# Which block of rows a partition takes: 4q+b takes 32b+q in place of 4q+b

## The chip, the core and the metric

The kernel runs on one core of one Trainium2 chip. The metric is the device time of one execution in microseconds (us), taken on the chip. Beside it stands a profile of one execution, in which every instruction of the engines and every packet of the DMA engines has its times. The engines used are VectorE (DVE), ScalarE (ACT), GpSimd (POOL, for constants and the end only) and SyncE (SP), which issues DMAs. TensorE does nothing here.

## The reference

The input has 32 x 512 rows of 1024 floats, and each row is summed:

```python
x = np.random.randn(32, 512, 1024).astype(np.float32)

def reference(x):
    return np.sum(x, axis=-1).astype(np.float32)
```

That is 16,384 sums over 67.1 MB that have to be read once. The output is 64 KB.

## The kernel before

The 16,384 rows are split over 128 partitions, J = 128 rows for each (lines 115 to 128). The split has two regions. The first P * BIG = 2,048 rows are region a: partition p takes BIG = 16 consecutive rows. The other 14,336 rows are region b: partition p takes LONG = 112 consecutive rows, a block of 448 KB. So consecutive partitions read places 448 KB apart in region b and 64 KB apart in region a. `rows_from` (line 131) gives the source of a load of n rows per partition from row j on: region b for j under 112, region a from there.

A load brings n rows of every partition into a tile of 16 rows (64 KB) per partition; the pool `in` has three such tiles. `rows` (line 188) issues one load on SP's queue and the sums that belong to it. The order is written out by hand (`manual_schedule`), and it is this:

1. One load of FIRST = 7 rows from region b, which `issue_first_load_at_entry` (line 10) moves to the very entry of the program, ahead of the barrier at which the engines meet.
2. Seven loads of 16 rows (line 215): the one of region a first, then region b at rows 16, 32, up to 96. The first of them is held until a tiny ACT instruction has run (line 222), the second until DVE has summed the first load (line 224). From the third on a load waits for a tile to come free.
3. The remaining rows 7 to 15 of region b: a load of 6 rows, one of 2, and the last row in two pieces of 560 and 464 floats (lines 227 to 237), each by a DMA of its own.

The sums land in a tile `sums` of 128 x 128, one column for each row of a partition. Most loads are summed by one DVE instruction over the tile (`vec`, line 151). The last ones are summed row by row, on DVE by an instruction that adds the two halves of a row and accumulates (`halves`, line 164), and on ACT by a copy that accumulates (`act`, line 177).

Three stores bring `sums` out. ACT's queue issues columns 16 to 111 (region b) and columns 112 to 127 (region a), both held until the two-row load has been summed (lines 239 and 240). SP's queue issues columns 0 to 15 of region b last (line 243), after the last sum. `wait_for_the_store_at_the_clear` (line 55) puts the wait for that last store at the instruction that clears the semaphores at the very end, on POOL. `order_waits` (line 31) only sorts the waits of an instruction that has several.

The change touches the views `x_a`, `x_b`, `out_b` and the loads and stores that use them.

Of the kernel before, what the change touches and what calls it, by code (L numbers as in the profile page):

```python
# [100 lines left out]
@with_exitstack  # L101
def kernel(
    ctx: ExitStack,
    tc: tile.TileContext,
    x: bass.AP,
    out: bass.AP,
):
    nc = tc.nc
    nc.at_finalize(issue_first_load_at_entry)
    nc.at_finalize(order_waits)  # L110
    nc.at_finalize(wait_for_the_store_at_the_clear)
    fp32 = mybir.dt.float32
    P = 128
    batch, seq, dim = x.shape
    rows = batch * seq
    J = rows // P
    BIG = 16

    LONG = J - BIG
    rows_in = x.flatten_outer_dims()
    rows_out = out.rearrange("b s -> (b s)")
    x_a = rows_in[: P * BIG].rearrange("(p j) d -> p j d", p=P)
    x_b = rows_in[P * BIG :].rearrange("(p j) d -> p j d", p=P)
    out_a = rows_out[: P * BIG].rearrange("(p j) -> p j", p=P)
    out_b = rows_out[P * BIG :].rearrange("(p j) -> p j", p=P)


    def rows_from(j, n):
        return x_b[:, j : j + n, :] if j < LONG else x_a[:, j - LONG : j - LONG + n, :]

    last = 0
    FIRST = 7
    pieces = (560, 464)
    LINE = 64

    with (
        tc.tile_pool(name="small", bufs=1) as smallpool,  # L140
        tc.tile_pool(name="in", bufs=3) as inpool,
        tc.tile_pool(name="unread", bufs=4, space=bass.MemoryType.PSUM) as upool,
        tc.tile_pool(name="stage", bufs=1) as stpool,
        tc.manual_schedule(),
    ):


        seed = smallpool.tile([P, LINE // 2], fp32)
        sums = stpool.tile([P, J], fp32)

        def vec(dst, src):
            return nc.vector.tensor_reduce(  # L152
                out=dst, in_=src, axis=mybir.AxisListType.X, op=mybir.AluOpType.add
            )

        def hold(inst, until, reason):
            tc.add_manual_dep(
                inst.ins,
                until.ins.name,
                mybir.DependencyInfo(mybir.DependencyClass.Sync, mybir.DependencyReason.DATA),  # L160
                reason=reason,
            )

        def halves(dst, src):
            n = src.shape[-1] // 2
            return nc.vector.tensor_tensor_reduce(  # L166
                out=src[:, :n],
                in0=src[:, :n],
                in1=src[:, n:],
                scale=1.0,  # L170
                scalar=0.0,
                op0=mybir.AluOpType.add,
                op1=mybir.AluOpType.add,
                accum_out=dst,
            )

        def act(dst, src, n):
            unread = upool.tile([P, dim], fp32)
            nc.scalar.activation(  # L179
                out=unread[:, :n],  # L180
                in_=src,
                func=mybir.ActivationFunctionType.Copy,
                accum_out=dst,
            )

        sums_of = []

        def rows(t, a, n, j, n_act, pairs=False):
            nv = n - n_act
            block = t[:, a * dim : (a + n) * dim].rearrange("p (n d) -> p n d", d=dim)  # L190
            load = nc.sync.dma_start(out=block, in_=rows_from(j, n))  # L191
            if pairs:
                for q in range(nv):
                    sums_of.append(halves(sums[:, j + q : j + q + 1], block[:, q, :]))
            else:
                sums_of.append(vec(sums[:, j : j + nv], block[:, :nv, :]))
            for q in range(nv, n):
                act(sums[:, j + q : j + q + 1], block[:, q, :], dim)
            return load

        def store(eng, dst, j0, j1):
            return eng.dma_start(out=dst, in_=sums[:, j0:j1])

        nc.vector.memset(seed[:, :1], 0.0)  # L204
        unread = upool.tile([P, dim], fp32)
        ready = nc.scalar.activation(  # L206
            out=unread[:, :1], in_=seed[:, :1], func=mybir.ActivationFunctionType.Copy
        )

        j = last  # L210
        t = inpool.tile([P, BIG * dim + LINE], fp32)
        rows(t, 0, FIRST, j, 0)
        first = sums_of[-1]
        wholes = [LONG, *range(BIG, LONG, BIG)]
        for k, at in enumerate(wholes):
            t = inpool.tile([P, BIG * dim + LINE], fp32)
            if k < len(wholes) - 1:
                load = rows(t, 0, BIG, at, 0)
            else:
                rows(t, 0, BIG, at, 7, pairs=True)  # L220
            if k == 0:
                hold(load, ready, "no second load while the first one's descriptors are made")
            if k == 1:
                hold(load, first, "no descriptors of later loads while the first ones start")

        t = inpool.tile([P, BIG * dim + LINE], fp32)
        rows(t, FIRST, 6, j + FIRST, 2, pairs=True)
        two = rows(t, FIRST + 6, 2, j + FIRST + 6, 1, pairs=True)
        a = BIG - 1

        j += a
        c, width = pieces
        whole = t[:, a * dim + c : BIG * dim + 2]
        nc.vector.memset(whole[:, width + 1 :], 0.0)  # L234
        part = t[:, a * dim : a * dim + c]
        nc.sync.dma_start(out=part, in_=rows_from(j, 1)[:, 0, :c])  # L236
        nc.sync.dma_start(out=whole[:, :width], in_=rows_from(j, 1)[:, 0, c:])
        late = "its packets come behind those of the loads"
        hold(store(nc.scalar, out_b[:, BIG:], BIG, LONG), two, late)
        hold(store(nc.scalar, out_a, LONG, J), two, late)  # L240
        halves(whole[:, width : width + 1], part)
        halves(sums[:, j : j + 1], whole)
        store(nc.sync, out_b[:, :BIG], 0, BIG)


# [28 lines left out]
```

## Time and profile before

| | |
|---|---|
| median of 3 runs | 161.14 us (161.13 to 161.27) |
| span of the profiled execution, first to last instruction | 159.5 us |
| median less that span, taken for what lies around it | 1.6 us |
| DVE busy | 120.6 us (76%) |
| ACT busy | 12.1 us (8%) |
| POOL busy | 0.2 us |
| read from memory | 67.11 MB, 421 GB/s over the span |
| chain that ended last | DMA 71%, DVE 27% |

The runs give times without a profile; the profiled execution has its span alone, which starts with SP's first DMA issue. A DMA has three times: the issue on the engine that starts it (SPq and ACTq in the views), its packets on the 16 DMA engines, and its landing, when its semaphore has its full count and a waiting engine goes on. In the views a windows row gives a stretch of the span with the busy time of each engine, the share of the 16 DMA engines' time that packets took (a packet is counted where it begins, so short stretches can pass 1) and the GB/s. The chain of work lists what the end of the program waited for, back to the start. Where DVE waits, the view puts it down to the DMA that it waited for.

### The profile page before, as it was taken

Reading aid. Unit: us, or ns where it says so; the run is one execution under the profiler, and the core shown is the slowest. Engines: PE = TensorE matmul, PEld = TensorE weight load, DVE = VectorE, ACT = ScalarE, POOL = GpSimd, SP = SyncE. Lnnn points to the kernel's source line nnn. Section 1 sums busy time; section 2 is a strip of 40 time slices with the busy share of each in tenths; the row PEclk is TensorE's granted clock in tenths of the full one; section 3 lists DMA queues with packets and bytes.
Section 4 is the critical chain, followed back from the end, with each engine's and each line's share of the span. In section 5 each row is a group of like instructions: output and inputs, shape, how many; then the busy total and the mean of one; then the engine's idle time right before and its main releaser. Section 6 shows DMA issues by size and latency. Waiting matters only on the chain.

```text
span 159.5 us, 135 instructions
## 1 busy us (share of the span) xinstructions
DVE 120.6 (76%) x41; ACT 12.1 (8%) x22; POOL 0.2 (0%) x4
## 2 busy tenths in 40 slices
DVE  0029600499995999769996899949999499994955
ACT  3000000000000000000000000000000000003993
POOL 0000000000000000000000000000000000000000
DMA  8899899699699699699699798996996996996993
GB/s 302 388 493 526 362 427 526 296 493 526 263 526 526 263 526 526 263 526 493 296 526 444 345 526 378 411 526 296 493 526 263 526 526 263 526 526 265 425 382 128
DMA packets 2160, 67.18 MB, mean 421 GB/s; under 512 B 624, under 2 KB 752, under 8 KB 880
## 3 DMA queue, kind: packets, MB, share of 16 engines
q1 hardware_dynamic: 1872, 67.12, 97.8%
q10 hardware_dynamic: 288, 0.06, 0.2%
HBM read 67.11 MB, written 0.07 MB: 421 GB/s over the span
## 4 chain that ended last, share of the span: by engine, by line
DMA 71%; DVE 27%; SPq 1%; issue 0%; DVEq 0%
DMA t<-in_x_dram 71%; DVE sums L152 26%; SPq L191 0%; SPq L236 0%; DVE t L166 0%; DVEq L269 0%
## 5 line engine op out<-in xcount | busy, mean ns | idle before, releaser
L152 DVE TENSOR_REDUCE sums<-t 128x16 f32<-128x16384 f32 (+1 forms) x7 | 110.9, 15849 | 32.3 <-DMA t<-in_x_dram 32.3
L179 ACT ACTIVATE unread<-t 128x1024 f32<-128x1024 f32 x10 | 10.1, 1011 | 144.3 <-DMA t<-in_x_dram 144.3
L166 DVE CUSTOM_DVE_ANT_0 t<-t 128x512 f32<-128x512 f32 (+2 forms) x16 | 9.6, 654 | 4.0 <-DMA t<-in_x_dram 4.0
L179 ACT ACTIVATION_READ_ACCUMULATOR unread<-t 128x1 f32 x10 | 1.9, 188 | 0.0
L206 ACT ACT_TABLE_LOAD x1 | 1.3, 1283 | 0.8 <-PEq L258 0.8
L166 DVE DVE_READ_ACCUMULATOR2_ANT sums<- 128x1 f32 x15 | 1.2, 82 | 0.0
L204 DVE MEMSET seed<- 128x1 f32 x1 | 0.1, 59 | 0.8 <-PEq L258 0.8
L206 ACT ACTIVATE unread<-seed 128x1 f32<-128x1 f32 x1 | 0.2, 174 | 0.0
L258 POOL MEMSET const-bfloat16-1.0<- 128x1 bf16 x1 | 0.1, 102 | 0.0
L258 POOL MEMSET const-uint8-127<- 128x1 uint8 x1 | 0.1, 102 | 0.0
L258 POOL MEMSET const-float32-0.0<- 128x1 f32 x1 | 0.1, 99 | 0.2 <-issue 0.2
L258 POOL MEMSET const-float32-1.0<- 128x1 f32 x1 | 0.1, 99 | 0.0
L166 DVE DVE_READ_ACCUMULATOR2_ANT t<- 128x1 f32 x1 | 0.1, 83 | 0.0
L234 DVE MEMSET t<- 128x1 f32 x1 | 0.1, 59 | 0.0
## 6 DMA issues: line engine op xcount, KB each, us to landing
t<-in_x_dram SPq DMA_DIRECT2D x1, 3584.0 KB, 11.0
t<-in_x_dram SPq DMA_DIRECT2D x1, 3072.0 KB, 28.7
t<-in_x_dram SPq DMA_DIRECT2D x1, 1024.0 KB, 30.7
t<-in_x_dram SPq DMA_DIRECT2D x1, 280.0 KB, 31.0
t<-in_x_dram SPq DMA_DIRECT2D x1, 232.0 KB, 31.1
t<-in_x_dram SPq DMA_DIRECT2D x7, 40.7
out_dram<-sums ACTq DMA_DIRECT2D x1, 48.0 KB, 1.6
out_dram<-sums ACTq DMA_DIRECT2D x1, 8.0 KB, 1.6
```

The costliest lines, as they stand in the source:

```text
L152: return nc.vector.tensor_reduce(out=dst, in_=src, axis=mybir.AxisListType.X, op=mybir.AluOpType.add)
L166: return nc.vector.tensor_tensor_reduce(out=src[:, :n], in0=src[:, :n], in1=src[:, n:], scale=1.0, scalar=0.0, op0=mybir.AluOpType.add, op ...
L179: nc.scalar.activation(out=unread[:, :n], in_=src, func=mybir.ActivationFunctionType.Copy, accum_out=dst,)
L204: nc.vector.memset(seed[:, :1], 0.0)
L206: ready = nc.scalar.activation(out=unread[:, :1], in_=seed[:, :1], func=mybir.ActivationFunctionType.Copy)
L234: nc.vector.memset(whole[:, width + 1 :], 0.0)
L258: nc = _bacc.Bacc("TRN2", target_bir_lowering=False, num_devices=1)
```

## The change

In region b partition p = 4q + b now takes block 32b + q, with b from 0 to 3 and q from 0 to 31. Partitions 0, 1, 2 and 3 take blocks 0, 32, 64 and 96, partitions 4 to 7 take 1, 33, 65 and 97, and so on. Neighbours in a group of four are 32 blocks or 14 MiB apart, and one group starts 448 KB behind the group before. Region a is as it was. The views are written as a source of 32 by 4 blocks of contiguous floats in place of 128 blocks of rows; the output of region b gets the same order. `cols_from` gives any run of floats of a partition's block, so that the last two pieces can be cut out of it. Nothing else differs: the sizes and the order of loads, sums and stores are the same.

```diff
+    SPREAD = 4
...
-    x_a = rows_in[: P * BIG].rearrange("(p j) d -> p j d", p=P)
-    x_b = rows_in[P * BIG :].rearrange("(p j) d -> p j d", p=P)
+    x_a = rows_in[: P * BIG].rearrange("(p j) d -> p (j d)", p=P)
+    x_b = rows_in[P * BIG :].rearrange("(b q j) d -> q b (j d)", b=SPREAD, j=LONG)
     out_a = rows_out[: P * BIG].rearrange("(p j) -> p j", p=P)
-    out_b = rows_out[P * BIG :].rearrange("(p j) -> p j", p=P)
+    out_b = rows_out[P * BIG :].rearrange("(b q j) -> q b j", b=SPREAD, j=LONG)
+
+    def cols_from(j, c, n):
+        at = j * dim + c
+        return x_b[:, :, at : at + n] if j < LONG else x_a[:, at - LONG * dim : at - LONG * dim + n]
 
     def rows_from(j, n):
-        return x_b[:, j : j + n, :] if j < LONG else x_a[:, j - LONG : j - LONG + n, :]
+        return cols_from(j, 0, n * dim)
...
-            load = nc.sync.dma_start(out=block, in_=rows_from(j, n))
+            load = nc.sync.dma_start(out=t[:, a * dim : (a + n) * dim], in_=rows_from(j, n))
...
-        nc.sync.dma_start(out=part, in_=rows_from(j, 1)[:, 0, :c])
-        nc.sync.dma_start(out=whole[:, :width], in_=rows_from(j, 1)[:, 0, c:])
+        nc.sync.dma_start(out=part, in_=cols_from(j, 0, c))
+        nc.sync.dma_start(out=whole[:, :width], in_=cols_from(j, c, width))
...
-        hold(store(nc.scalar, out_b[:, BIG:], BIG, LONG), two, late)
+        hold(store(nc.scalar, out_b[:, :, BIG:], BIG, LONG), two, late)
...
-        store(nc.sync, out_b[:, :BIG], 0, BIG)
+        store(nc.sync, out_b[:, :, :BIG], 0, BIG)
```

## The prediction

> **What bounds the kernel now.** I read the DMA part of the page first, because the kernel only reads 67.11 MB and adds it up.
>
> ```profile
> ## 3 DMA queue, kind: packets, MB, share of 16 engines
> q1 hardware_dynamic: 1872, 67.12, 97.8%
> ```
>
> One queue, q1 (SP's), keeps the 16 DMA engines busy for 97.8% of the span. Whether that is a ceiling or only a queue that is never empty shows in the windows, cut at the starts of the reductions. The columns are the window, its length, busy time of DVE, ACT and POOL, the clock, the DMA share (1.00 is all 16 engines) and GB/s.
>
> ```profile
> 11.03:30.30 19.27, 7.62 (x1) 0.00 (x0) 0.00 (x0) 1.00 1.01 435
> 30.30:49.62 19.32, 17.22 (x1) 0.00 (x0) 0.00 (x0) 1.00 1.00 434
> ...
> 107.58:126.90 19.32, 17.22 (x1) 0.00 (x0) 0.00 (x0) 1.00 1.00 434
> ```
>
> Each window of about 19.3 us is one 8.39 MB load, always at 433 to 435 GB/s, although DVE needs only 17.22 us of it. The packet records agree: a 64 KB packet takes 2.418 us at the median and 2.448 at most, on every engine, with no gap behind it. So an engine moves 65,536 / 2.418 = 27.1 bytes per ns, and its 4 MiB (a sixteenth of x) take 154.75 us. The load of the 16-row region has its blocks 64 KB apart, the others 448 KB apart, and both run at this rate.
>
> The chain of work (start, length, what) says what lies around these 154.75 us. I take its first piece and its end.
>
> ```profile
> 0.00 11.01 DMA t<-in_x_dram
> ...
> 126.16 31.13 DMA t<-in_x_dram
> 157.30 0.02 issue
> 157.32 0.40 DVE t L166
> 157.72 0.01 DVEq L269
> ```
>
> The reads end at 157.30, one short DVE reduction follows, and then comes SP's store. At the start a cut of the windows at 0.99 us shows that nothing moves yet:
>
> ```profile
> 0.00:0.99 0.99, 0.06 (x1) 0.23 (x1) 0.20 (x4) 1.00 0.00 0
> ```
>
> SP's first issue runs from 0 to 0.36; the packet records begin at 1.00 on the first engine and 1.34 on the last (mean 1.13). The first 28 KB packet of an engine takes 1.53 to 2.11 us (mean 1.78) where the later ones take 1.06: 0.72 us of start-up. Now 1.13 + 0.72 + 154.75 = 156.60 us; the engines end their data between 156.46 and 156.94. The whole span is thus a start of about 1.9 us, a stream at its ceiling, and an end of 2.2 us. Work inside the stream is free. The start and the end are not.
>
> The two issue lines (line, engine, operation, count, then shortest, median and longest issue in ns, first and last start in us):
>
> ```profile
> L191 SPq DMA_DIRECT2D t<-in_x_dram x10: 327/328/435, 0.0 to 125.2; - x10
> ```
> ```profile
> L202 ACTq DMA_DIRECT2D out_dram<-sums x2: 374/450/525, 156.1 to 156.5; - x2
> ...
> L202 SPq DMA_DIRECT2D out_dram<-sums x1: 348/348/348, 157.8 to 157.8; - x1
> ```
>
> An SP issue that stands alone takes 0.33 to 0.36 us, one right behind another 0.43, and the slowest in the trace 0.525 (ACT's second).
>
> **The change part by part.** It has two effects: the addresses, and the form of the transfers.
>
> *Bytes, packets, engine work: zero.* Each partition still takes 112 consecutive rows, so a packet stays a contiguous 64 KB run and there are as many. The order of instructions on DVE, ACT, POOL and SP is the same, one for one, with the same waits. No wait is added. DVE and ACT see the same tiles.
>
> *Form of the transfers.* A plain step over 128 blocks becomes two steps, 32 by 4. Thirteen of the 15 DMAs get it: the eleven loads from the 112-row region, ACT's 96-column store and SP's 16-column store. The load and the store of the 16-row region stay plain. In the built program 15 DMAs carry a mark named for a precooked issue before, and only these two after. What the mark is worth, and what a three-dimensional issue costs, no row of before shows. I exclude a gain, as the instruction describes the same runs with one more step. The nearest rows bound the extra time of one issue: 0 if it costs the same; 0.20 if it becomes like the slowest issue (0.525 against 0.33); 0.35 if the sequencer does as much again as now. Since the mark is lost as well as a step added, I take a value between the last two, 0.275 us.
>
> Where it lies:
> - First load: nothing else can move before it. The first packet goes from 1.00 to 1.28 and the whole stream behind it moves along: +0.275 on the path.
> - Six 16-row loads, issued at 18.68, 19.06 and then every 19.3 us from 47.55 to 105.55, each when DVE frees a buffer. At 18.68 the load ahead still runs to 30.30, 11.6 us; at the others, as at 47.55, the rest of one load and a whole one behind it are queued, over 20 us. Hidden by those; with only one buffer the 0.275 would show each time.
> - The last four loads at 124.82 to 126.60: 4 x 0.275 = 1.1 us later, behind a load that ends at 146.28. Hidden by 20 us.
> - ACT's stores: the first is 0.275 longer, so the second, queued behind it on ACT, starts later as well. It lands 1.6 us after its start at 156.46, at 158.1, and SP's store lands 1.4 us after 157.76, at 159.16. Hidden by 1.1 us. Nothing else stands behind it on ACT but the final barrier.
> - SP's last store: everything but the final clear is done. +0.275 on the path. SP's final barrier work behind it moves along and still ends (158.83 now) before the landing.
>
> Sum: 2 x 0.275 = +0.55 us. By the bounds 0 to +0.70.
>
> *Addresses at start-up.* The first packets of the 16 engines read other places. Their 0.72 us of extra time can shrink or grow. If all were as good as the best (1.53), the mean falls by 0.25; if all were as bad as the worst (2.11), it rises by 0.33. No row says which, so I take 0 and keep both ends.
>
> *Addresses in the stream.* Neighbouring partitions, 448 KB apart now, will be 14 MiB apart. The rate was the same at 64 KB and at 448 KB, and it is the engine's own: 0. The trace has no row at 14 MiB; that is the second rival.
>
> The profiled execution has a span of 159.5 (159.49), and 1.65 us around it make the median of 161.14. 159.49 + 0.55 = 160.04, and with the same 1.65 that is 161.69, so **161.7 us**, +0.34%.
>
> **The rivals.**
>
> *The issue's form costs nothing that shows* (0 to 0.1 each), so that the start-up packets alone decide: 161.14 -0.25 to +0.33, likeliest 161.1, not slower. For it: a DMA issue might be a fixed sum whatever the pattern. Against it: the issues in this trace vary from 327 to 525 ns, so they are not fixed. It decides when the first issue stays at 0.36. With the best start-up on top, and the engines' ends (156.46 to 156.94) drawn together to their mean, another -0.28, it reaches 160.6: faster.
>
> *Reads collide.* If blocks a multiple of 2 MiB apart share a part of the memory, an engine that moves on to its next block while the others still read meets them there. Low price: every packet at the slowest now seen, 2.448 against a mean of 2.419, over 56 packets of 64 KB per engine is +1.6 us: with the issues 163.3. High price: each of the 56 pays the 0.72 of a cold first packet: +40 us, 202. For it: 14 MiB is seven times 2 MiB, the roundest step in this kernel. Against it: if an engine takes four neighbouring partitions in turn, the 16 blocks in flight at one time are then 448 KB apart instead of 1.75 MiB, closer than before. It decides as soon as packets pass 2.45 us.
>
> The Trainium skill, page "DMA: Bandwidth & Descriptors", section "Latency and other measured facts", speaks against the change here: it gives 207 GB/s at a row pitch of 512 KiB per partition, 164 at 2 MiB and 103 at 4 MiB. Its ratio 207/164 on the 154.75 us would be an estimate of about +41 us. No run here shows it yet. The section "The descriptor swizzle" of the page gives each engine partitions 4e to 4e+3 and their like 32 further on, by which the streams side by side are the near ones; I therefore give this rival little.
>
> *The transfers are divided in another way among the engines*, since one side now has 32 outermost steps and the other 128. Packets of some engines would then be longer or the engines end far apart. I price it like the collision, and put it in the same case.
>
> **How the numbers follow.** Issue cost at both ends: 0.64 (161.2 to 162.2, point 161.7). No visible cost: 0.25, of which 0.08 comes out faster by over 0.2%. Collision or another division: 0.11. About 0.2%, 0.3 us, is what a measurement of this kernel tells from no change; that is 160.82 to 161.46. Of the forecast case 0.09 falls below 161.46. So slower 0.64 - 0.09 + 0.11 = 0.66, same 0.26, faster 0.08. The range from 160.9 to 162.6 takes in both bounds of the issue with the start-up's and leaves out the collision and the best start.
>
> **What would show it.** SP's first issue at 0.5 to 0.7 us instead of 0.36 and the first packet at about 1.28; SP's store at about 0.62 instead of 0.348; the plain second load still at 0.33, as its own control; windows of the stream still at 434 GB/s with packets of 2.42 us. Wrong: issues unchanged, the longer issue without a later first packet, or a stream under 430 GB/s.

## The result and the profile after

The changed kernel takes 162.2 us (162.15 to 162.26, four runs) against 161.2 (161.13 to 161.28): a ratio of 1.006, 95% interval 1.0048 to 1.0072, slower by 1.0 us. Its profiled execution has a span of 160.47 us against 159.49, so the trace holds 0.98 us of it.

The DMA part of the page for the kernel after:

```profile
## 3 DMA queue, kind: packets, MB, share of 16 engines
q1 hardware_dynamic: 1872, 67.12, 97.3%
```

There are as many packets and bytes as before, at a slightly lower share of a longer span. The windows, cut again at the starts of the reductions (window, its length, busy DVE, ACT, POOL, clock, DMA share, GB/s):

```profile
11.33:30.63 19.30, 7.62 (x1) 0.00 (x0) 0.00 (x0) 1.00 1.00 435
30.63:49.98 19.35, 17.22 (x2) 0.00 (x0) 0.00 (x0) 1.00 1.00 434
...
107.97:127.29 19.32, 17.22 (x1) 0.00 (x0) 0.00 (x0) 1.00 1.00 434
```

The stream runs at the 433 to 435 GB/s of before. What is new stands at its edges. Before, packets moved from 1.00 on; now nothing moves until 1.42:

```profile
0.00:0.99 0.99, 0.00 (x0) 0.00 (x0) 0.20 (x4) 1.00 0.00 0
0.99:1.42 0.43, 0.05 (x1) 0.12 (x1) 0.00 (x0) 1.00 0.00 0
```

The chain of work after (start, length, what):

```profile
0.00 11.30 DMA t<-in_x_dram
...
127.09 30.76 DMA t<-in_x_dram
157.85 0.02 issue
157.88 0.40 DVE t L171
158.28 0.01 DVEq L274
```

The reads end at 157.85, 0.56 us later than before (157.30), and the reduction takes the same 0.40. The issue lines of loads and stores (shortest, median and longest issue in ns, first and last start):

```profile
L196 SPq DMA_DIRECT2D t<-in_x_dram x10: 356/535/655, 0.0 to 125.8; - x10
```
```profile
L207 ACTq DMA_DIRECT2D out_dram<-sums x2: 597/612/627, 156.6 to 157.3; - x2
...
L207 SPq DMA_DIRECT2D out_dram<-sums x1: 609/609/609, 158.3 to 158.3; - x1
```

The longest load issue, 655 ns, is the first (361 before). The shortest, 356, is the plain load of the 16-row region. SP's store is issued in 609 ns (348 before), and from the start of its issue to its landing the trace has 1.84 us (1.42 before).

So 0.56 us is lost ahead of the end of the reads and 0.42 after it: 0.98 in all, which is the whole growth of the span.

| start and end, us | before | after |
|---|---|---|
| first issue on SP | 0.361 | 0.655 |
| first packets of the 16 engines: first, mean, last start | 1.00, 1.11, 1.34 | 1.42, 1.67, 2.39 |
| length of these packets, mean | 1.78 | 1.66 |
| last landing of the reads | 157.30 | 157.85 |
| SP's store: issue, start to landing | 0.348, 1.420 | 0.609, 1.839 |

(The start column is counted over the 16 earliest 28 KB packets; the mean is 1.11, where the prediction wrote 1.13.)

### The profile page after: what moved, and what is told of

Same layout as the page of the kernel before. It is cut to its first block, busy times and chain, and to the rows that moved or that the text cites. A ratio compares the mean times of both kernels' runs of the same rounds, so it can differ in the third digit from the quotient of the medians.

```text
span 160.5 us, 135 instructions
## 1 busy us (share of the span) xinstructions
DVE 120.6 (75%) x41; ACT 12.1 (8%) x22; POOL 0.2 (0%) x4
## 4 chain that ended last, share of the span: by engine, by line
DMA 71%; DVE 26%; SPq 1%; issue 0%; DVEq 0%
DMA t<-in_x_dram 71%; DVE sums L157 26%; SPq L196 1%; SPq L241 0%; DVE t L171 0%; DVEq L274 0%
```

## The experiments

The mark is the one that the prediction speaks of: the built program puts it, for a precooked issue, on a transfer with a plain pattern. The third step is the one that the form of 32 by 4 blocks adds. Two theories were set against each other. **Form:** a transfer without the mark, and with a third step, is slower to issue and to turn into packets, and this shows at both ends. **Addresses:** the reads are later because of where they go. Times of before differ a little, as each set of runs has its own. The signed figures after a time, like +0.62, are us against before.

| kernel | time, us | before, us | ratio, 95% interval |
|---|---|---|---|
| loads of the change, stores of before | 161.85 | 161.23 | 1.0038 (1.0025 to 1.0050) |
| stores of the change, loads of before | 161.70 | 161.23 | 1.0029 (1.0018 to 1.0040) |
| before, all 15 transfers unmarked | 161.91 | 161.23 | 1.0044 (1.0031 to 1.0056) |
| before, first load unmarked | 161.59 | 161.24 | 1.0026 (1.0017 to 1.0035) |
| 32 by 4 form, nearly the addresses of before | 161.66 | 161.23 | 1.0025 (1.0014 to 1.0035) |
| 32 by 4 form, 7 MiB inside a group | 161.88 | 161.24 | 1.0043 (1.0026 to 1.0059) |
| 16-row region at both ends, 32b+q | 161.44 | 161.25 | 1.0007 (0.9998 to 1.0016) |
| 16-row region at both ends, 4q+b | 161.40 | 161.25 | 1.0006 (0.9997 to 1.0014) |
| groups of 2 | 162.28 | 161.24 | 1.0062 (1.0049 to 1.0075) |
| groups of 8 | 307.79 | 161.25 | 1.9071 (1.9043 to 1.9098) |
| 16 by 8 form, nearly the addresses of before | 308.28 | 161.24 | one run |
| groups of 16 | 581.45 | 161.25 | one run |

### One part of the change at a time

The loads of the change with the stores of before (an edit of the changed kernel; the two stores get the slices of before with it):

```diff
-    out_b = rows_out[P * BIG :].rearrange("(b q j) -> q b j", b=SPREAD, j=LONG)
+    out_b = rows_out[P * BIG :].rearrange("(p j) -> p j", p=P)
...
```

> The loads of the changed kernel with the stores of the kernel before: the sums are the same, but those of the 112-row region go to other places of the output. The trace after the change puts +0.56 us at the start (last landing of the reads 157.30 to 157.85) and +0.42 us at the end (last store, issue to landing, 1.42 to 1.84). Theory form: the issue and the making of descriptors of a transfer without the mark cost this at both ends; this kernel should keep the first part only, 161.2 + 0.56 = 161.75 us, with SP's first issue at 0.655, first packets at 1.4 and the last store's issue back at 0.35. Theory addresses: the reads are late because of where they go, and then the whole difference of 1.0 us stays, 162.2.

Measured: 161.85 us, +0.62.

```profile
L196 SPq DMA_DIRECT2D t<-in_x_dram x10: 355/535/612, 0.0 to 126.0; - x10
...
L207 SPq DMA_DIRECT2D out_dram<-sums x1: 357/357/357, 158.3 to 158.3; - x1
```

The first issue takes 0.612 us, the first packets start at 1.39, the reads land last at 157.87, and the store is back at an issue of 0.357 and a landing after 1.42. The start of the change is kept and its end is gone.

The other half, with `out_b` of the change in the kernel before:

> The loads of the kernel before with the stores of the changed one: the sums of the 112-row region go to other places of the output. Theory form: only the end is longer, by 0.42 us, 161.6 us; last landing of the reads at 157.3 as before, the last store's issue at 0.61 and its landing 1.84 after its start. Theory addresses (of the reads): as before, 161.2.

Measured: 161.70 us, +0.47.

```profile
L202 SPq DMA_DIRECT2D out_dram<-sums x1: 632/632/632, 157.9 to 157.9; - x1
```

The store takes 0.632 us to issue and 1.86 to land. In this execution the reads land last at 157.45, 0.15 later than before, though the loads are those of before, so one trace is no finer than that. The two halves add up to 1.09 us, against 1.0 for the whole; their intervals reach some 0.2 us to each side. Within that, the whole is the sum of a start and an end.

### The mark alone

```diff
     nc = tc.nc
+    nc.dge_precook = False
```

This makes the built program leave the mark off; patterns and addresses stay those of before.

> The kernel before with all of its patterns plain (128 blocks) and its addresses, but all 15 transfers without the mark of the built program. Theory form, by the mark: +0.9 to +1.0 us, 162.1 to 162.2, first issue near 0.65, first packet near 1.4. Theory form, by the third dimension: the mark is worth little, 161.2 to 161.4, first issue at 0.36 to 0.45. Theory addresses: 161.2 with an issue that may be longer.

Measured: 161.91 us, +0.68. This lies between the two forms of the theory, and neither had it. The issue lines of its loads and of its last store:

```profile
L192 SPq DMA_DIRECT2D t<-in_x_dram x10: 471/472/601, 0.0 to 125.6; - x10
...
L203 SPq DMA_DIRECT2D out_dram<-sums x1: 509/509/509, 158.1 to 158.1; - x1
```

An unmarked plain issue that stands alone takes 472 ns, where before has 328 and the change 535: of the 207 ns that the change adds, 144 go with the mark and 63 with the third step. The first issue is 0.538, the first packet starts at 1.33 (mean 1.56), the store is issued in 0.509 and lands after 1.745. So the mark is about two thirds of the whole, 0.68 of 1.0 us. The third step and the new places share the rest, some 0.3.

With the mark taken from the first load alone (the same line before that load, and the opposite one behind it):

> The kernel before with the mark taken from its first load alone. All transfers unmarked were +0.68 us, of which the trace puts 0.30 at the start (last landing 157.60 against 157.30) and 0.33 at the end (last store, issue to landing 1.745 against 1.42). Theory form: the start alone, 161.25 + 0.3 to 0.35 = 161.55 to 161.6 us, first issue at 0.54 and first packet at 1.33. If the unmarked loads of the middle take part: less than 0.15 us here.

Measured: 161.59 us, +0.35, as expected.

```profile
L191 SPq DMA_DIRECT2D t<-in_x_dram x10: 327/328/544, 0.0 to 125.7; - x10
```

Here only the longest issue, the first, has changed, 361 to 544 ns. The profiled execution took 161.85 us, 0.26 more than the median of this kernel, so its trace is not used for the size of the loss. The rest of the +0.68 is 0.33 us, which is what the store's landing moved by (1.42 to 1.745). The other eleven loads, unmarked in the first of the two kernels, cost nothing that shows.

### The form at the addresses of before, and the addresses without the form at the ends

This is again an edit of the changed kernel, with the stores of before:

```diff
-    x_b = rows_in[P * BIG :].rearrange("(b q j) d -> q b (j d)", b=SPREAD, j=LONG)
+    x_b = rows_in[P * BIG :].rearrange("(q b j) d -> q b (j d)", b=SPREAD, j=LONG)
+    x_b = bass.AP(x_b.tensor, x_b.offset, [x_b.ap[0], [(LONG - 1) * dim, SPREAD], x_b.ap[-1]])
...
```

> Loads in the form of the changed kernel (32 by 4 steps, no mark), but at nearly the addresses of the kernel before: the step inside a group of four is one row short of a block, so that the two steps can't be merged, and some partitions sum rows shifted by one to three. Stores as before. Theory form: the same as the loads alone, 161.75 us, with packets of 64 KB at 2.42 us. Theory addresses: the start is back to that of before, 161.2 to 161.5, although the issue is long.

Measured: 161.66 us, +0.43.

```profile
L197 SPq DMA_DIRECT2D t<-in_x_dram x10: 352/536/627, 0.0 to 125.7; - x10
```

The first issue takes 0.627 us, the first packets start from 1.40 on (mean 1.54), and the reads land last at 157.73. So the form brings most of the loads' part with the places of before. The loads of the change have +0.62. Run against run, in the same set, the five times with the new places (161.71 to 161.92) lie almost wholly above the seven with the old ones (161.61 to 161.82), so about 0.2 us of the loads' part probably goes with the places. No run shows by what, and the next two kernels show nothing of it in the middle of the stream.

Next the region whose pattern is plain goes to both ends and the 112-row region into the middle, once with each block order. The edit of the changed kernel:

```diff
-    last = 0
+    last = LONG
...
-        wholes = [LONG, *range(BIG, LONG, BIG)]
+        wholes = [*range(0, LONG, BIG)]
...
-        hold(store(nc.scalar, out_b[:, :, BIG:], BIG, LONG), two, late)
-        hold(store(nc.scalar, out_a, LONG, J), two, late)
+        hold(store(nc.scalar, out_b, 0, LONG), two, late)
...
-        store(nc.sync, out_b[:, :, :BIG], 0, BIG)
+        store(nc.sync, out_a, LONG, J)
```

> The block order of the change (partition 4q+b takes block 32b+q), but the 16-row region, whose pattern is plain, is read and stored at both ends, and the 112-row region in the middle: seven of the loads and ACT's store keep the 32 by 4 form, the first load, the last four and SP's last store are plain and marked. Theory form: nothing of the cost shows, 161.1 to 161.3 us, with middle issues at 0.53 us and packets at 2.42. Theory addresses: the reads of the middle are slower by the new places, packets above 2.43 us on the mean, over 161.5 us.

> The same reordering of the regions with the block order of the kernel before, all 15 less one transfers plain and marked (one store on ACT in place of two): the control for the run with 32b+q. Theory form: 161.1 to 161.3, the same as that one. Theory addresses: this one 161.1 to 161.3 and that one slower.

Measured: 161.44 and 161.40 us, a little above the range given for both, and alike. Neither is told from before (1.0007 and 1.0006, intervals around 1).

```profile
L196 SPq DMA_DIRECT2D t<-in_x_dram x10: 334/535/616, 0.0 to 125.3; - x10
...
L207 SPq DMA_DIRECT2D out_dram<-sums x1: 348/348/348, 157.8 to 157.8; - x1
```

With 32b+q the seven loads of the middle are issued in 0.53 to 0.62 us as in the change, their 64 KB packets take 2.419 us on the mean, and the issue of the store at the end takes 0.348. To within some 0.1 us the new block order costs nothing in the stream, and the longer issue costs nothing where a load is queued ahead of it. None of the kernels tried is faster than the one before.

### Larger and smaller groups: the division among the engines

> The changed kernel with groups of eight: partition 8q+b takes block 16b+q, the form is 16 by 8 and neighbours are 7 MiB apart. Theory form: the same as the changed kernel, 162.1 to 162.3, since the issue has the same third step. Theory addresses or another division among the engines: the start or the packets differ from those of the changed kernel, and the time by over 0.3 us.

Measured: 307.8 us, nearly twice the time. Windows of the kernel with groups of eight, same columns:

```profile
78.20:118.60 40.40, 17.22 (x1) 0.00 (x0) 0.00 (x0) 1.00 1.01 209
118.60:158.90 40.30, 17.22 (x1) 0.00 (x0) 0.00 (x0) 1.00 1.00 207
```

All 16 engines are busy (share 1.00), but they move 207 to 209 GB/s; the packet records have 64 KB packets of 5.1 us at the median in place of 2.418. The same execution holds its own control: while the plain load of the 16-row region passes, from 20.4 to 38.4 us, its packets take 2.42 us and the engines move 411 GB/s.

> The changed kernel with groups of sixteen: the source has 8 outermost steps by 16. This tests the rival that the transfers are divided otherwise among the engines. The Trainium skill, page DMA: Bandwidth & Descriptors, section Why a DMA increments its semaphore by 16 and not by 1, says that the engines of a transfer are the largest number up to 16 that divides the outermost steps of both sides, so 8 here. By that, 8 engines carry 58.7 MB of the 112-row region and their half of the rest of 8.4 MB: 7.86 MB each at 27.1 bytes per ns is 290 us, with the start and the end 294 us. If all 16 engines take part whatever the outermost step: 162.2 us.

Measured: 581 us, twice what was expected. Windows of the kernel with groups of sixteen:

```profile
145.40:222.70 77.30, 17.22 (x1) 0.00 (x0) 0.00 (x0) 1.00 0.50 109
222.70:299.30 76.60, 17.22 (x1) 0.00 (x0) 0.00 (x0) 1.00 0.50 109
```

Half of the engines' time is taken (share 0.50), and the packet records have eight packets at a time. That is as the Trainium skill says, on the page "DMA: Bandwidth & Descriptors", section "Why a DMA increments its semaphore by 16 and not by 1", which the expectation names. But each engine is at half its speed too (5.0 us at the median), which the expectation had not reckoned with.

Whether the places in memory or the division does this was asked with two kernels. One has the 16 by 8 form at nearly the places of before, the same edit as above with `SPREAD = 8`:

> The 16 by 8 form, which takes about twice the time, at nearly the addresses of the kernel before (blocks 448 KB apart, the step inside a group of eight one row short; some partitions sum rows shifted by one to seven). Stores as before. Theory division: with 16 outermost steps each of the 16 engines gets eight neighbouring partitions, and two engines meet at the way into the same partitions: packets of 5.05 us and about 306 us again. Theory addresses: the 7 MiB between blocks were the cause, and here packets are back at 2.42 us and the time at 161.7.

```profile
78.20:118.60 40.40, 17.22 (x1) 0.00 (x0) 0.00 (x0) 1.00 1.00 208
118.60:158.90 40.30, 17.22 (x1) 0.00 (x0) 0.00 (x0) 1.00 1.01 208
```

Measured: 308.3 us, 208 GB/s. The other has the 32 by 4 form with 7 MiB between the blocks of a group (`[16 * LONG * dim, SPREAD]` as its second step), with the stores of before:

> The counterpart: the 32 by 4 form of the change with 7 MiB between the blocks of a group, as in the 16 by 8 run. Blocks overlap, so that partitions sum other rows, some rows several times and others not at all; the bytes read are as many. Stores as before. Theory division: packets of 2.42 us and 161.7 to 161.9 us, as the loads of the change alone. Theory addresses: packets of 5 us, about 306 us.

```profile
69.00:88.30 19.30, 17.22 (x1) 0.00 (x0) 0.00 (x0) 1.00 1.00 435
```

Measured: 161.88 us, 435 GB/s. So it is the form, and not the distance, that halves the rate with groups of eight. Groups of sixteen were not tried at other distances. The Trainium skill, page "SBUF — State Buffer", section "Door 1: The DMA port swizzle (why [64,N] ≈ [32,N])", has an account: partitions come in fours, four partitions share one of 16 ways in with the four that lie 32 further on, and 8 or 4 of these ways carry some 218 or 109 GB/s. The measured 207 to 209 and 109 agree. That an engine takes its eight or sixteen partitions in order, so that engines meet at such a way, is inferred: the trace has no partitions. Nor does any run show why 32 by 4, which also leaves eight partitions to each engine, is free of it.

Groups of two:

> The changed kernel with groups of two: form 64 by 2, neighbours 28 MiB apart. Theory form, with the division sound as long as a group is four partitions or fewer: 162.1 to 162.3 us, packets at 2.42 us. Theory addresses: 28 MiB is four times 7 MiB, and packets are slower than those of the change.

Measured: 162.28 us, as the change. Packets of 64 KB take 2.421 us on the mean with 28 MiB between neighbours.

## Why the prediction held, and which term was too small

- *What bounds the kernel.* This was right. The stream is a ceiling of the engines, 434 GB/s before and after, and only the start and the end could move.
- *The form.* This was right in kind. The issue term was 0.275 us: measured +0.294 for the first load and +0.261 for the store. The plain load of the 16-row region stayed near its 0.33 (0.356).
- *The sum, +0.55 us.* It was little more than half of what was measured, +0.98 in the trace and +1.0 in the times. The step that failed is "the first packet goes from 1.00 to 1.28 and the whole stream behind it moves along", and the same for the store. It took all that follows an issue to keep its distance. In fact the first packet started at 1.42 and the last engine's first at 2.39 in place of 1.34, and the store's landing moved by 0.42 where its issue grew by 0.26. So the longer issue is only some half of what the change costs; the rest comes between the issue and the packets or the landing. Why it is spent there no trace shows. The bound of 0.70 was taken from issue rows alone, and fell short for that reason.
- *Start-up, taken as 0 with -0.25 to +0.33.* The first packets were 0.12 us shorter on the mean, on engines that started 0.55 later. Executions differ here: plain, marked first loads began on their last engine at 1.34 before, at 1.70 with the stores of the change, and at 1.94 with the 16-row region at both ends and 4q+b. So these traces show no address effect at the start; the times of the loads at old and new places leave room for one of about 0.2 us.
- *Hidden parts.* This was right. ACT's second store landed at 158.97, 1.2 us ahead of SP's at 160.15, and the loads of the middle cost nothing.
- *Rival: no visible cost.* It is refuted by its own sign, the first issue: 0.655 us in place of 0.361.
- *Rival: reads collide.* It is refuted at 14 MiB, at 7 and at 28, where 64 KB packets keep their 2.42 us. The rule for row pitches in the Trainium skill (page "DMA: Bandwidth & Descriptors", section "Latency and other measured facts"), which by its ratio was an estimate of +41 us, is not borne out here. The Trainium skill has it from copies between HBM tensors with 16 KiB for each partition, which the prediction left out; these are loads with runs of 64 KB, and for them the measurement decides. From the section "The descriptor swizzle" of the same page the prediction took the numbering of the first eight engines for that of all; the Trainium skill has the other eight start at partition 64. The streams side by side are near ones by either numbering. The rival was to win when packets pass 2.45 us. In the profiled execution of the change 24 of 896 did, up to 2.535, and the mean was 2.4222 in place of 2.4195, which is 56 x 0.0027 = 0.15 us for an engine. But the loads of the change without its stores have 2.420. At the old addresses, before with its first load unmarked has 2.424, and the 32 by 4 form near the places of before has 2.422 with packets up to 2.613. So this is scatter between executions and not the new places.
- *Rival: another division.* It did not happen at 32 by 4, but the runs with 16 by 8 and 8 by 16 show that it exists, one step further, at +147 and +420 us. It was priced with the collision at up to +40; that price was much too low for those two forms.

The range, 160.9 to 162.6, held because it was made from several cases; the forecast case's own range ended at 162.2, where the result lies. Both upper bounds together, 0.70 for the issues and 0.33 for the start-up, give 161.14 + 1.03 = 162.17, and the 0.4 above that was not derived. Since the 0.4 us that the issues did not cover came from a term that the sum did not have, the range held in part by luck.

## What to carry to other kernels

In a kernel like this one, which streams at the DMA engines' rate, a transfer's form counts where nothing is queued ahead of it: at the first load and the last store. There price the time from issue to first packet or to landing, not the issue alone. When a new order of blocks needs two steps in place of one, give the ends to a region that stays plain, and look at the GB/s of one window before trusting the division among the engines: 32 by 4 kept 434, 16 by 8 fell to 208.

## What the runs showed of the hardware that was not expected

- An SP issue that stands alone takes 0.328 us marked, 0.472 unmarked and plain, 0.535 unmarked with 32 by 4 steps.
- An unmarked first load has its first packet 1.33 us after its issue began, in place of 1.00; an unmarked store of 8 KB lands 1.745 us after, in place of 1.42.
- The same 67 MB with the same packet sizes takes 162, 308 or 581 us as the outermost count of the source is 32, 16 or 8.
